# A float32 encoder layer on one core: the second chunk's global attention heads in query blocks of 512 instead of 256

## The chip, the core and the metric

One core of a Trainium2 chip runs the whole program. The metric is the device time of one execution in microseconds (us). The engines are PE (matmuls; PEld is its weight load), DVE (elementwise work on 128 partitions), ACT (activations and copies), POOL (here the reductions over partitions) and SP (issues the DMAs). Each engine goes through its own list of instructions in the order that the build has fixed; semaphores tie the lists together.

## What is computed

Two sequences, 1024 and 256 tokens with 16 meta tokens put before each, go through one layer of width 2048. A norm and one projection give q, k, v and a gate z for 8 global heads (a: 2 shared k and v, with rotary embedding) and 8 local heads (b: a window of 8 x 16 keys with a bias). Then one output projection and the residual. Cut to the part that the change touches, the global attention:

```python
qg = qb.reshape(B, L, N_KV_A, G, HEAD_DIM)
s = jnp.einsum('blkgd,bskd->bkgls', qg, k).astype(jnp.float32) * scale
p = jax.nn.softmax(s, axis=-1).astype(v.dtype)
o = jnp.einsum('bkgls,bskd->blkgd', p, v)
...
ya = global_gqa(qa, ka, va) * jax.nn.silu(za)
```

## The kernel before, in words

Float32 products are made of three: each operand is split into a high part that PE takes as it is and a low remainder, and high x high, high x low and low x high are summed in PSUM. `split` (L64) does this with an ACT copy (`hi`, L66) and a DVE subtraction (`lo`, L67).

The tokens are worked in two chunks: chunk one holds the short sequence, the first 240 tokens of the long one and the meta tokens; chunk two the other 784 tokens. The projection goes by strips of 128 output columns (`strips`, L192): for each of 16 tiles of the model width and each of two token blocks (512 and 272 in chunk two) three matmuls (L227 to L229) add to a PSUM tile `pp`, of which there are 4, so two strips of chunk two fit. A strip is then evacuated: `qk_evac` (L257) for q and k, with up to six tiles of the pool `ev` for each block (8 tiles in all), `z_evac` (L299) for the gate, `v_rows` and `rows_out` (L287, L530) for v.

Chunk two's global heads are the loop in `chunk2` (L941 to L953): for each of the 8 heads a strip for z, one for q, then `run` (L879), which attends, then `fill`, which puts one strip of the local heads behind as filling. There is one tile each for k, v, q and z (one buffer), so the next head's q can be written only when this head's last score matmul has read it. `run` calls `attend` (L366) for four blocks of 256 queries. A block has 8 key tiles of 128; two of them share one PSUM bank (`sp`, 2 banks) and one score buffer (`S`, pool `s`, 5 buffers of 128 x 512):

- scores: three matmuls for each key tile (L377 to L379), an ACT copy to `S` (L381), a running maximum on DVE from the second pair on (L385, L387); then two matmuls for the meta keys (`meta_scores`, L312; Sl on ACT at L319, Sm on DVE at L320);
- maximum over the two halves (L392) and with the meta scores (L326), then over the partitions on POOL (L328);
- probabilities: subtraction on DVE (L397), exponential on ACT (L398), sum on DVE (L401, L403, L407, L343) and over the partitions on POOL (L346);
- values: each pair's probabilities are split into `ph` and `pl` (2 buffers each, pool `ph`), and three matmuls for each key tile (L418 to L420) and one for the meta values (L421) add to `po`; `put_y` (L349) divides by the sum, multiplies by the gate and stores.

Behind the global heads come the local heads (`attend_strip`, L463), tied to fixed places in the remaining strips, and then the output projection (L1068 to L1070).

The order on each engine is not written out by hand: the build simulates the engines with its own costs and lists each engine's instructions as they come free there, by the order of the code, with buffers and banks limiting what may run ahead. So changed tiles and buffers move instructions on every engine. The pools are opened in `build` (L1187): `work` (L1225) lists those that both kinds of attention share, L1236 opens them for the whole of chunk two.

## Time and profile before

| | |
|---|---|
| median of 3 runs | 2160.92 us (2160.66 to 2160.97) |
| profiled execution: its time | 2159.27 us |
| profiled execution: span | 2157.5 us |
| matmuls on PE | 11745 |
| first and last score matmul of the wide stage (L377) start at | 686.8 us and 1313.9 us |
| DVE busy in 760 to 840, 840 to 920, 920 to 1000 us | 75.03, 74.62, 73.24 of 80 us |
| ACT busy in the same | 60.19, 60.69, 58.92 of 80 us |
| clock granted to PE, mean | 1.00 |

How to read the views: busy time counts an instruction from its start to its end, and neighbours on one engine can overlap; PE's ends are modelled, so the distance from one matmul's start to the next says more than its duration. A row of groups gives line, engine, operation, the tiles written and read, shapes and count, then busy us and mean ns, then the engine's idle time ahead of them and what ended it. In the timeline a row is start, length, engine, line, operation; x4 means four such instructions in a row, taken together. The stage of the change runs from 686 to 1316 us.

### The profile page before, as it was taken

The page shows a single profiled execution, that of the slowest core. Times are in us where ns is not written, and L with a number is a line of the kernel's source. Part 1 is how long each engine was busy: PE and PEld are TensorE (multiplying, and loading weights), DVE is VectorE, ACT ScalarE, POOL GpSimd, SP SyncE. Part 2 cuts the span into 40 slices and gives each one's busy share as a digit, 9 for nine tenths or more (in the row PEclk, how much of TensorE's full clock was granted, in tenths as well). Part 3 has the DMA queues.
Part 4 walks back from the last instruction along what each step waited for, and adds up shares of the span by engine and source line. Part 5 has one row for each costly group of instructions (what it writes and reads, how often), then busy time and mean ns, then how long its engine had stood idle before and what let it go on. Part 6 is the DMA issues. An engine that isn't in the chain of part 4 may idle for free.

```text
span 2157.5 us, 33972 instructions
## 1 busy us (share of the span) xinstructions
PE 2151.3 (100%) x11745; PEld 1877.5 (87%) x11745; DVE 1658.5 (77%) x2989; ACT 1189.0 (55%) x2411; POOL 522.3 (24%) x250
## 2 busy tenths in 40 slices
PE   9999999999999999999999999999999999999999
PEld 7888888888888999999999999998989988888887
DVE  7698976788874899997799998677787886545763
ACT  7677644454565777776677775444443464232230
POOL 1142422222221223231143224324333311000000
PEclk9999999999999999999999999999999999999999
DMA  8666789988664333334332344654443364662663
GB/s 294 216 192 221 241 297 313 331 288 265 214 193 137 94 105 104 106 105 135 98 107 93 104 127 146 188 158 136 130 132 123 115 212 142 239 235 92 234 224 108
DMA packets 257420, 377.24 MB, mean 175 GB/s; under 512 B 43072, under 2 KB 108768, under 8 KB 257248
## 3 DMA queue, kind: packets, MB, share of 16 engines
q1 hardware_dynamic: 257248, 375.07, 53.6%
q8 instruction: 92, 1.51, 0.3%
q14 instruction: 80, 0.66, 0.1%
HBM read 281.01 MB, written 100.38 MB: 177 GB/s over the span
## 4 chain that ended last, share of the span: by engine, by line
PE 99%; DMA 0%; DVE 0%; SPq 0%; issue 0%; ACT 0%
PE pp L227 22%; PE pp L229 22%; PE pp L228 22%; PE pq L1069 6%; PE pq L1068 6%; PE pq L1070 6%; PE po L519 2%; PE sp L485 2%; PE sp L378 1%; PE sp L379 1%; PE sp L377 1%; PE po L420 1%; PE po L419 1%; PE po L418 1%; PE tp L540 0%; PE sp L430 0%
## 5 line engine op out<-in xcount | busy, mean ns | idle before, releaser
L227 PE MATMUL pp<-x,wh 128*128 128x512 f32 (+1 forms) x1664 | 655.0, 395 | 0.9 <-ACT wh L66 0.9
L229 PE MATMUL pp<-x,wl 128*128 128x512 f32 (+1 forms) x1664 | 647.6, 390 | 0.0
L228 PE MATMUL pp<-x,wh 128*128 128x512 f32 (+1 forms) x1664 | 647.1, 389 | 0.0
L229 PEld LDWEIGHTS pp<-x,wl 128*128 128x128 f32 x1664 | 312.4, 188 | 60.9 <-DVE wl L67 0.2
L227 PEld LDWEIGHTS pp<-x,wh 128*128 128x128 f32 x1664 | 312.3, 188 | 59.0 <-ACT wh L66 3.1
L228 PEld LDWEIGHTS pp<-x,wh 128*128 128x128 f32 x1664 | 312.8, 188 | 52.1
L67 DVE TENSOR_TENSOR wl<-wr,wh 128x512 fp32r<-128x512 f32 (+2 forms) x287 | 215.5, 753 | 122.2 <-ACT wh L66 91.3
L262 POOL PARTITION_ALL_REDUCE m<-ms x78 | 222.4, 2852 | 354.3 <-ACT ms L260 293.1
L346 POOL PARTITION_ALL_REDUCE tot<-a x80 | 179.2, 2240 | 435.4 <-DVE a L343 417.1
L66 ACT CAST wh<-wr 128x512 fp32r<-128x512 f32 (+2 forms) x287 | 173.7, 610 | 184.2 <-PE pp L228 170.4
L228 PE MATMUL pp<-xb,wh 128*128 128x272 f32 x832 | 240.7, 289 | 0.0
L227 PE MATMUL pp<-xb,wh 128*128 128x272 f32 x832 | 239.8, 288 | 0.0
L229 PE MATMUL pp<-xb,wl 128*128 128x272 f32 x832 | 239.1, 287 | 0.0
L328 POOL PARTITION_ALL_REDUCE ma<-m x80 | 114.4, 1429 | 448.4 <-DVE m L326 439.7
L1068 PE MATMUL pq<-wm,yh 128*128 128x512 f32 x560 | 218.3, 390 | 0.0
L1070 PE MATMUL pq<-wm,yl 128*128 128x512 f32 x560 | 218.2, 390 | 0.0
L1069 PE MATMUL pq<-wm,yh 128*128 128x512 f32 x560 | 218.0, 389 | 0.0
L227 PEld LDWEIGHTS pp<-xb,wh 128*128 128x128 f32 x832 | 156.5, 188 | 7.5
L228 PEld LDWEIGHTS pp<-xb,wh 128*128 128x128 f32 x832 | 156.5, 188 | 7.5
L229 PEld LDWEIGHTS pp<-xb,wl 128*128 128x128 f32 x832 | 157.4, 189 | 0.3
L1068 PEld LDWEIGHTS pq<-wm,yh 128*128 128x128 f32 x560 | 105.1, 188 | 21.8
L1070 PEld LDWEIGHTS pq<-wm,yl 128*128 128x128 f32 x560 | 105.1, 188 | 21.8
(214 smaller groups left out, 3932.1 us busy)
## 6 DMA issues: line engine op xcount, KB each, us to landing
wr<-in_w_in SPq DMA_DIRECT2D x413, 256.0 KB, 3.4
wld<-wl SPq DMA_DIRECT2D x132, 256.0 KB, 4.2
wl<-wld SPq DMA_DIRECT2D x132, 256.0 KB, 3.1
yr<-yd SPq DMA_DIRECT2D x35, 512.0 KB, 5.1
wq<-in_w_out SPq DMA_DIRECT2D x64, 256.0 KB, 5.0
td<-wq SPq DMA_DIRECT2D x64, 256.0 KB, 4.4
ww<-td SPq DMA_DIRECT2D x64, 256.0 KB, 5.2
ww<-in_w_out SPq DMA_DIRECT2D x48, 256.0 KB, 5.4
```

The source lines that it names most:

```text
L66: self.hi = nc.scalar.copy(hi, full).ins
L67: return nc.vector.tensor_tensor(out=lo, in0=full, in1=hi.bitcast(F32), op=ALU.subtract).ins
L227: nc.tensor.matmul(p[:, :n], wh[:, k, :], xh[:, :n], start=first, stop=False)
L228: nc.tensor.matmul(p[:, :n], wh[:, k, :], xl[:, :n], start=False, stop=False)
L229: self.lastmm = nc.tensor.matmul(p[:, :n], wl[:, k, :], xh[:, :n], start=False, stop=last).ins
L262: nc.gpsimd.partition_all_reduce(m2[:], ms[:], P, RED.add)
L328: nc.gpsimd.partition_all_reduce(ma[:], m1[:], P, RED.max)
L346: nc.gpsimd.partition_all_reduce(tot[:], a1[:], P, RED.add)
L485: nc.tensor.matmul(dst, k[:, o:o + P], qfv[:, a:e, :], start=True, stop=True)
L1068: nc.tensor.matmul(ps, yh, wh, start=k == 0, stop=False)
L1069: nc.tensor.matmul(ps, yh, wl, start=False, stop=False)
L1070: self.lastmm = nc.tensor.matmul(ps, yl, wh, start=False, stop=k == 7).ins
```

## The change

`run` calls a new function, `attend_wide`, for two blocks of 512 queries (`WB`) instead of `attend` for four of 256. Each key tile has a PSUM bank and a score buffer of its own, so that every matmul of these heads has 512 columns, and there is no halving step at the end of maximum and sum. The low parts `pl` are taken from the score buffers (`s`, now 9 buffers of the same size), the high parts `ph` keep two buffers. `y` is written over the sum's tile. The low meta probabilities have one tile of 512 columns (`Pw`) instead of two of 256. The wide heads' pools are closed before the local heads begin, and the local heads open theirs on the same memory. `po` has 512 columns everywhere, of which the others use 256. The diff, cut to its core:

```diff
@@ meta_scores
+        n = pm.shape[1]
+        sm = self.sm.tile([M3, n], F32, tag="Sm", name="Sm")
+        if n > QB:
+            sl = self.ph.tile([P, n], F32R, tag="ph", name="Sl", align_bytes=ALIGN)[:M3].bitcast(F32)
+        else:
+            sl = self.t.tile([P, n], F32, tag="t", name="Sl")[:M3]
...
@@ meta_probs
-        pm3 = self.pms[self.npm % 2]
+        pm3 = self.pms[self.npm % len(self.pms)]
...
@@ put_y
-        y = self.y.tile([P, QB], F32, tag="y", name="y")
+        y = tot if n > QB else self.y.tile([P, n], F32, tag="y", name="y")
...
+    def attend_wide(self, q, zs, keys, meta, vals, vmeta, ydst):
+
+        nc = self.nc
+        qh, ql = q[:, 0, :], q[:, 1, :]
+        S, mx = [], None
+
+        def bank(name):
+            return self.sp.tile([P, 2, QB], F32, tag="sp", name=name)[:].rearrange("p a b -> p (a b)")
+
+        for j, (kh, kl) in enumerate(keys):
+            ps = bank("sp")
+            nc.tensor.matmul(ps, kh, qh, start=True, stop=False)
+            nc.tensor.matmul(ps, kh, ql, start=False, stop=False)
+            nc.tensor.matmul(ps, kl, qh, start=False, stop=True)
+            s = self.s.tile([P, WB], F32, tag="S", name="S", align_bytes=ALIGN)
+            nc.scalar.copy(s[:], ps)
+            S.append(s)
+            if j == 1:
+                mx = self.mx.tile([P, WB], F32, tag="mx", name="mx")
+            if j:
+                nc.vector.tensor_tensor(out=mx[:], in0=(S[0] if j == 1 else mx)[:], in1=ps, op=ALU.max)
+        sm = self.meta_scores(bank("sm_ps"), meta, qh, ql, 1.0)
+        ma = self.all_max(mx, sm)
+        for j, s in enumerate(S):
+            nc.vector.tensor_tensor(out=s[:], in0=s[:], in1=ma[:], op=ALU.subtract)
+            nc.scalar.activation(s[:], s[:], AF.Exp, scale=SCALE)
+            if j == 1:
+                acc = self.mx.tile([P, WB], F32, tag="mx", name="acc")
+            if j:
+                nc.vector.tensor_tensor(out=acc[:], in0=(S[0] if j == 1 else acc)[:], in1=s[:], op=ALU.add)
+        pm3 = self.meta_probs(sm, ma, SCALE)
+        tot = self.all_sum(acc, sm)
+        po = self.op.tile([P, WB], F32, tag="po", name="po")[:]
+        for j, (s, (vh, vl)) in enumerate(zip(S, vals)):
+            ph = self.ph.tile([P, WB], F32R, tag="ph", name="ph", align_bytes=ALIGN)
+            pl = self.s.tile([P, WB], F32R, tag="S", name="pl", align_bytes=ALIGN)[:]
+            self.split(ph[:], pl, s[:])
+            nc.tensor.matmul(po, vh, ph[:], start=j == 0, stop=False)
+            nc.tensor.matmul(po, vl, ph[:], start=False, stop=False)
+            nc.tensor.matmul(po, vh, pl, start=False, stop=False)
+        nc.tensor.matmul(po, vmeta, pm3[:], start=False, stop=True)
+        self.put_y(po, tot, zs, ydst)
...
@@ chunk2, run
-            for b in range(4):
-                c = slice(QB * b, QB * b + QB)
+            for b in range(2):
+                c = slice(WB * b, WB * b + WB)
                 keys = [(k[:, 0, o:o + P], k[:, 1, o:o + P]) for o in range(0, NP, P)]
-                for _ in self.attend(q[:, :, c], z[:, c], keys, km, v, vm[:], self.yd[0][:, 2 * b:2 * b + 2, h, :]):
-                    pass
+                self.attend_wide(q[:, :, c], z[:, c], keys, km, v, vm[:], self.yd[0][:, 4 * b:4 * b + 4, h, :])
...
+        self.open_local()
         for f in (load_kq, load_v, load_z):
...
@@ build
-                for name, bufs in (("k", 1), ("v", 1), ("tab", 1), ("q", 1), ("z", 1), *work, ("y", 2), ("qf", 1)):
-                    pool(es_attn, name, bufs, **kw)
+                first = (("k", 1), ("v", 1), ("tab", 1), ("q", 1), ("z", 1))
+                es_wide = ExitStack()
+                for name, bufs in (*first, ("s", 9), ("mx", 2), ("t", 3), ("ph", 2), ("sm", 1), ("pw", 1)):
+                    pool(es_wide, name, bufs, **kw)
...
```

The order of instructions changes with it. PE at the end of global head 4 (counted from 0), from the meta scores (`sm_ps`) of its last block on; before (`pp` is a strip's PSUM, `x` and `xb` its tokens, `wh` and `wl` its weights):

```order
L315 MATMUL sm_ps_12031<-q_11445,km_10978 112x256
L316 MATMUL sm_ps_12031<-q_11445,km_10978 112x256
L227 MATMUL pp_13071<-x_6705,wh_13075 128x512
L228 MATMUL pp_13071<-x_6705,wh_13075 128x512
L229 MATMUL pp_13071<-x_6705,wl_13076 128x512
L227 MATMUL pp_13072<-xb_6682,wh_13075 128x272
L228 MATMUL pp_13072<-xb_6682,wh_13075 128x272
L229 MATMUL pp_13072<-xb_6682,wl_13076 128x272
L227 MATMUL pp_13072<-xb_6690,wh_13075 128x272
L228 MATMUL pp_13072<-xb_6690,wh_13075 128x272
L229 MATMUL pp_13072<-xb_6690,wl_13076 128x272
L227 MATMUL pp_13072<-xb_6698,wh_13075 128x272
```

and now, where `sp` is already the next head's scores (`q_11550`), `po` the sum of the values, and `ph` and `pl` the split probabilities:

```order
L316 MATMUL sm_ps_11157<-q_10764,km_10297 112x512
L317 MATMUL sm_ps_11157<-q_10764,km_10297 112x512
L441 MATMUL sp_11724<-q_11550,kf_10294 128x512
L441 MATMUL sp_11730<-q_11550,kf_10294 128x512
L442 MATMUL sp_11724<-q_11550,kf_10294 128x512
L443 MATMUL sp_11724<-q_11550,kf_10294 128x512
L442 MATMUL sp_11730<-q_11550,kf_10294 128x512
L443 MATMUL sp_11730<-q_11550,kf_10294 128x512
L467 MATMUL po_11198<-ph_11199,va_10616 128x512
L468 MATMUL po_11198<-ph_11199,va_10617 128x512
L469 MATMUL po_11198<-pl_11200,va_10616 128x512
```

Before, a strip's matmuls stand behind the meta scores, and the block's own first value matmul comes 82 rows behind the first of them; now it stands directly behind the next head's first six score matmuls, and the next strip's matmuls come behind the values.

DVE at the same place, the last rows up to the block's last low part; before (`acc` is the running sum, `Pm` the low meta probabilities, `a1` the sum of the halves, `mx` the next block's maximum; `t`, `rs_l` and `rs_r0` belong to the evacuation of a strip):

```order
L67 TENSOR_TENSOR pl_12076<-S_12007,ph_12075 128x512
L274 TENSOR_TENSOR t_12555<-t_12555,ts_12557 128x272
L403 TENSOR_TENSOR acc_12047<-acc_12047,S_12028 128x512
L338 TENSOR_TENSOR Pm_270<-Sm_12034,Pm_270 16x256
L407 TENSOR_TENSOR a1_12059<-acc_12047 128x256
L385 TENSOR_TENSOR mx_12593<-S_12582,sp_12584 128x512
L343 TENSOR_TENSOR a1_12059<-a1_12059,Sm_12034 16x256
L81 TENSOR_TENSOR rs_l_12565<-m2_12552,rs_l_12565 128x272
L67 TENSOR_TENSOR pl_12086<-S_12018,ph_12085 128x512
L82 SCALAR_TENSOR_TENSOR rs_r0_12567<-rs_l_12565,rs_r0_12567 128x272
L277 TENSOR_TENSOR rs_r0_12567<-t_12555,rs_r0_12567 128x272
L67 TENSOR_TENSOR pl_12096<-S_12028,ph_12095 128x512
```

and now:

```order
L68 TENSOR_TENSOR pl_11221<-S_11126,ph_11220 128x512
L459 TENSOR_TENSOR acc_11171<-acc_11171,S_11133 128x512
L82 TENSOR_TENSOR rs_l_12177<-m2_12174,rs_l_12177 128x512
L68 TENSOR_TENSOR pl_11228<-S_11133,ph_11227 128x512
L459 TENSOR_TENSOR acc_11171<-acc_11171,S_11140 128x512
L68 TENSOR_TENSOR pl_11235<-S_11140,ph_11234 128x512
L83 SCALAR_TENSOR_TENSOR rs_r0_12179<-rs_l_12177,rs_r0_12179 128x512
L459 TENSOR_TENSOR acc_11171<-acc_11171,S_11147 128x512
L68 TENSOR_TENSOR pl_11242<-S_11147,ph_11241 128x512
L264 TENSOR_TENSOR m2_12188<-m2_12188,eb2_321 128x272
L281 SCALAR_TENSOR_TENSOR rs_r0_12179<-pp_12050,nqkw_245,rs_r0_12179 128x512
L68 TENSOR_TENSOR pl_11249<-S_11154,ph_11248 128x512
```

The four low parts of a block have become eight, and the evacuation of the waiting strip (`pp_12050`) stands between them.

More of the change, by code (lines that the diff above doesn't have):

```diff
@@ L351, in put_y @@
         nc = self.nc
[L352 removed]
+        n = tot.shape[1]
+        r = self.t.tile([P, n], F32, tag="t", name="r")
         nc.scalar.activation(r[:], tot[:], AF.Ln)
@@ new lines, in attend @@
+        nc.tensor.matmul(po, vmeta, pm3[:], start=False, stop=True)
[37 more added lines that the diff above has]
+            nc.tensor.matmul(po, vh, pl, start=False, stop=False)
+        nc.tensor.matmul(po, vmeta, pm3[:], start=False, stop=True)
@@ L456, in attend_sample @@
         yield
-        po = self.op.tile([P, QB], F32, tag="po", name="po")
-        nc.tensor.matmul(po[:], vmeta, pm3[:], start=True, stop=False)
+        po = self.op.tile([P, WB], F32, tag="po", name="po")[:, :QB]
+        nc.tensor.matmul(po, vmeta, pm3[:], start=True, stop=False)
         for i in range(2):
@@ L514, in attend_strip @@
         yield
-        po = self.op.tile([P, QB], F32, tag="po", name="po")
-        nc.tensor.matmul(po[:], vmeta, pm3[:], start=True, stop=False)
+        po = self.op.tile([P, WB], F32, tag="po", name="po")[:, :QB]
+        nc.tensor.matmul(po, vmeta, pm3[:], start=True, stop=False)
         for t in (0, 3, 1, 2):
@@ L565, in meta_tiles @@
         self.npm = 0
-        self.pms = [self.mt.tile([P, QB], F32R, tag=f"Pm{i}", name="Pm") for i in range(2)]
+        self.pms = self.pms_narrow = [self.mt.tile([P, QB], F32R, tag=f"Pm{i}", name="Pm") for i in range(2)]
         self.vm3s = [self.mt.tile([P, P], F32R, tag="vm", name="vm3")]
@@ L1235, in build, with open_local @@
                 pool(es_proj, "ev", 8, side="right", **kw)
-                for name, bufs in (("k", 1), ("v", 1), ("tab", 1), ("q", 1), ("z", 1), *work, ("y", 2), ("qf", 1)):
-                    pool(es_attn, name, bufs, **kw)
+                first = (("k", 1), ("v", 1), ("tab", 1), ("q", 1), ("z", 1))
+                es_wide = ExitStack()
+                for name, bufs in (*first, ("s", 9), ("mx", 2), ("t", 3), ("ph", 2), ("sm", 1), ("pw", 1)):
+                    pool(es_wide, name, bufs, **kw)
+                self.pms = [self.pw.tile([P, WB], F32R, tag="Pw", name="Pm")]
+                nc.gpsimd.memset(self.pms[0][:].bitcast(F32), 0.0)
+                def open_local():
+                    es_wide.close()
+                    self.pms = self.pms_narrow
+                    for name, bufs in (*first, *(x for x in work if x[0] != "ph"), ("y", 2), ("qf", 1)):
+                        pool(es_attn, name, bufs, **kw)
+                self.open_local = open_local
                 self.chunk2()
```

25 lines of the change are left out of this document (11 added, 14 removed).

## The prediction

> **What bounds the kernel now.** I read the page first, then the list of waits, then the stage of the change in the table of stretches, then single instructions in the timeline. The profiled execution took 2159.27 us, 1.77 more than its span of 2157.5. First line of the page, and the chain that ended last by engine:
>
> ```profile
> PE 2151.3 (100%) x11745; PEld 1877.5 (87%) x11745; DVE 1658.5 (77%) x2989; ACT 1189.0 (55%) x2411; POOL 522.3 (24%) x250
> PE 99%; DMA 0%; DVE 0%; SPq 0%; issue 0%; ACT 0%
> ```
>
> All that PE ever waited for, of the whole run, in the view of the waits (total, times, longest):
>
> ```profile
> PE warm L633 <- DVE wz L630: 1.2, 1, 1.2
> PE pp L227 <- ACT wh L66: 0.9, 2, 0.6
> PE tp L296 <- DVE vt L289: 0.3, 1, 0.3
> ```
>
> PE bounds every stage; nothing else ever holds it up. So the change can gain only by shortening PE's own work, and loses each microsecond by which PE now waits. Chunk two's global heads, then its local heads, in the table of stretches (length; busy time and count of PE, PEld, DVE, ACT, POOL):
>
> ```profile
> 686.00:1316.00 630.00, 630.00 (x4089) 577.39 (x4088) 551.75 (x1002) 453.00 (x917) 175.43 (x88) 1.00 0.35 106
> 1320.00:1800.00 480.00, 480.00 (x2840) 431.70 (x2839) 373.51 (x793) 226.94 (x506) 163.31 (x87) 1.00 0.48 153
> ```
>
> DVE is busy 551.75 of 630 us (88%): it keeps up, with little to spare. What matters is how much other work PE has in its queue while an attention block passes through DVE.
>
> **Part by part. The wider matmuls.** Counts by form, before (the first and the last of six like rows, L418 to L420 and L377 to L379):
>
> ```profile
> L420 PE MATMUL po<-pl,va 128*128 128x256 f32 x256 | 71.9, 281 | 0.0
> ...
> L377 PE MATMUL sp<-q,kf 128*128 128x256 f32 x256 | 70.8, 282 | 0.0
> ```
>
> With the three meta matmuls of each of the 32 blocks (L315, L316, L421) that is 6 x 256 + 96 = 1632 matmuls of 256 columns; they become 816 of 512. Durations overlap, so the price is the distance of starts, in the timeline:
>
> ```profile
> 1171.80 0.40 PE L228 MATMUL pp<-x,wh 128*128 128x512 f32 x1
> ...
> 1173.88 0.39 PE L228 MATMUL pp<-x,wh 128*128 128x512 f32 x1
> ...
> 1175.34 0.28 PE L378 MATMUL sp<-q,kf 128*128 128x256 f32 x1
> ...
> 1175.94 0.28 PE L378 MATMUL sp<-q,kf 128*128 128x256 f32 x1
> ```
>
> Nine steps of 512 columns in 2.08 us are 0.231 each; five of 256 in 0.60 are 0.120. A pair saves 0.009 us, 816 pairs 7 us (5 to 9, as starts are given to 0.01 us). The Trainium skill, TensorE: Matmul & The Clock Gate, section Back-to-back issue gap, gives N / 2.4 + 2.5 ns, by which a pair would save 2.5 ns and all pairs 2 us; the distances above show more, and the measurement decides.
>
> **The waits that come in.** A block now holds eight score buffers through subtraction, exponential and split; nine exist, and each low part takes one. The next block's first scores need the buffer of this block's eighth tile, so blocks follow one another instead of overlapping. The last score copies of the next head stand behind the last split, and that head's q, of which there is one tile, is written only when this head's last scores are done. A strip's results then queue for the eight ev tiles behind q's, its PSUM banks stay taken, and PE has no projection to run. The order of instructions shows the outcome. Behind the last score matmul of the second block of heads 1, 4 and 5 (counted from 0) PE has only the next head's first six score matmuls and then the value matmuls, each waiting for DVE; the first projection is the 33rd instruction. Before, projections stood there.
>
> How long until DVE releases it? From the meta scores to the seventh low part stand Sl on ACT and 33 DVE instructions: 29 of 512 elements, 4 of 272, the same in the three places. Durations, by form in the stretch of these heads:
>
> ```profile
> L67 DVE TENSOR_TENSOR pl<-S,ph 128x512 fp32r<-128x512 f32 x124 | 91.6, 750 | 7.0 <-ACT ph L66 4.3 <-PE po L420 2.5
> L397 DVE TENSOR_TENSOR S<-S,ma 128x512 f32<-128x512 f32 x124 | 78.6, 696 | 6.2 <-POOL ma L328 6.0
> L403 DVE TENSOR_TENSOR acc<-acc,S 128x512 f32<-128x512 f32 x62 | 45.6, 735 | 1.2 <-ACT S L398 0.8
> L387 DVE TENSOR_TENSOR mx<-mx,sp 128x512 f32<-128x512 f32 x64 | 43.7, 682 | 18.2 <-ACT S L381 17.3
> L82 DVE SCALAR_TENSOR_TENSOR rs_r<-rs_l,rs_r 128x512 f32<-128x512 f32 x13 | 11.8, 911 | 0.3
> L263 DVE TENSOR_TENSOR m<-m,eb 128x512 f32<-128x512 f32 x13 | 9.7, 750 | 0.0
> L81 DVE TENSOR_TENSOR rs_l<-m,rs_l 128x512 f32<-128x512 f32 x13 | 9.5, 727 | 3.3 <-ACT rs_l L80 3.3
> L277 DVE TENSOR_TENSOR rs_r<-t,rs_r 128x272 f32<-128x272 f32 x8 | 7.1, 885 | 0.1
> L81 DVE TENSOR_TENSOR rs_l<-m,rs_l 128x272 f32<-128x272 f32 x13 | 6.5, 499 | 2.0 <-ACT rs_l L80 2.0
> L67 DVE TENSOR_TENSOR q<-rs_r,q 128x272 fp32r<-128x272 f32 x7 | 5.9, 847 | 0.7 <-ACT q L66 0.7
> L82 DVE SCALAR_TENSOR_TENSOR rs_r<-rs_l,rs_r 128x272 f32<-128x272 f32 x12 | 5.1, 427 | 0.0
> ```
>
> By these means: 8 subtractions 5.6, 7 low parts 5.3, 6 sums 4.4, 5 small ones of 512 columns (taken as L387) 3.4, L263, L81 and L82 2.4, the four of 272 columns 2.7, together 23.8 us; Sl adds 0.58 (the copy of 128x512 below), 24.3 in all. The four of 272 cover the all-reduce of the maximum, estimated at twice the 1.37 us of 256 columns at most:
>
> ```profile
> L381 ACT COPY S<-sp 128x512 f32<-128x512 f32 x126 | 72.8, 581 | 47.8 <-PE sp L379 43.3 <-DVE pl L67 3.2
> L328 POOL PARTITION_ALL_REDUCE ma<-m x31 | 42.5, 1372 | 131.0 <-DVE m L326 122.3 <-ACT wh L211 5.2 <-DMA wl<-wld 3.5
> ```
>
> Means hold overlap: DVE starts come closer. One block of before in the timeline, from its meta scores to its last low part:
>
> ```profile
> 1143.79 0.28 PE L316 MATMUL sm_ps<-q,km 128*112 128x256 f32 x1
> ...
> 1144.96 0.41 DVE L320 SCALAR_TENSOR_TENSOR Sm<-sm_ps,Sl 48x256 f32<-48x256 f32 x1
> 1145.29 0.41 DVE L392 TENSOR_TENSOR m<-mx 128x256 f32<-128x256 f32 x1
> ...
> 1147.55 2.50 DVE L397 TENSOR_TENSOR S<-S,ma 128x512 f32<-128x512 f32 x4
> 1149.97 0.41 DVE L333 TENSOR_TENSOR Sm<-Sm,ma 48x256 f32<-48x256 f32 x1
> ...
> 1161.91 0.68 DVE L67 TENSOR_TENSOR pl<-S,ph 128x512 fp32r<-128x512 f32 x1
> ```
>
> Four subtractions in 2.42 us are 0.605 each, 256 columns 0.33. At that pace the 33 take 29 x 0.605 + 4 x 0.35 = 18.9 us, with Sl and some 0.6 of the all-reduce left open 20.1. The block shown decides which is nearer: from L320 on it has 17 instructions of 512 columns and 10 of 256, 13.6 us by starts, 16.4 by means; it took 17.6. So I take the means. PE's work up to there is 29 matmuls at 0.231, 6.7 us. PE stands 24.3 - 6.7 = 17.6 us, at least 20.1 - 6.7 = 13.4. I take 17, three times: 51 us (40 to 54).
>
> The same count for the other 13 blocks: PE's queue is short by 4.6, 3.6, 4.6 and 2.0 us in the second blocks of heads 0, 2, 3 and 6 by means, by 0.6, 0, 1.5 and 0 by starts: 2 to 15 us, and I take 8, the middle, since waits in so short a gap may also fall elsewhere. In the other nine blocks PE has 3.6 to 5.7 us to spare by means, so they cost nothing while that cover holds. Counted so, every block of before has 1.6 us or more to spare, which fits its empty list of waits.
>
> After a stop PE may start slowly. At the kernel's start nine matmuls of 512 columns show it:
>
> ```profile
> 1.17 4.02 PE L633 MATMUL warm<-wz 128*128 128x512 bf16 x9 [1.17 <-DVE wz L630]
> ```
>
> That is 0.447 each instead of 0.231, 1.9 us lost on nine. I put 2 us on each of the three long stops, 6 us (0 to 9: during a stop a value matmul runs now and then). The Trainium skill, TensorE: Matmul & The Clock Gate, section Why this matters for your kernels, says that a gap of some 3 us between bursts puts PE back to half its clock; the nine matmuls agree with a half clock at the start, and no run here shows it after a gap yet.
>
> **Edits put at nothing.** DVE's sums and maxima go from 2 x 3 to 7 instructions, but the halves' L392 and L407 go away and the instructions on few partitions halve in number; all is off PE's chain except where counted. One Pm tile instead of two: its next writer comes a block later, some 40 us. The local heads' own pools wait for the wide ones; their first scores stand 46 us of PE work behind the last wide scores. Local heads now start later and share less time: DVE is 78% busy there (373.51 of 480), and in the order their scores still lead their values by 15 us of PE work or more, but for the last head, whose order stays as it was. If that cover failed I would add 10 us.
>
> **Sum.** 2159.3 - 7 + 51 + 8 + 6 = 2217.3 for the profiled execution; the median of the runs lies 1.65 us above it (2160.92), so 2219.
>
> **Rivals.** First, the waits are covered and only the matmuls count: 2160.9 - 7 = 2154, faster. Before's rows speak for it (PE never waited, though DVE was as busy), the order speaks against it: PE and DVE each go through their queue in order, so 6.7 us of PE work can hide at most as much of DVE's. It decides from the point where DVE gets to the seventh low part within 6.7 us. Chance 0.04; another 0.02 for gain and waits that cancel within 0.2%.
>
> Second, DVE goes at its pace of starts and the short gaps close by themselves: - 9 + 40 with no slow start, 2160.9 + 31 = 2192 and up to 2203. For it: DVE has no one to wait for in the three places. Against: the block shown took 17.6. Chance 0.22.
>
> Third, the ring of nine buffers makes first blocks wait as well. They have 3.6 to 5.7 us to spare by means; if DVE's own waits, which made the block shown 1.2 us longer than its means, grow with twice the tiles and more to 7 us, eight blocks lose some 2 to 3 each, 20 us: 2239 and above. Chance 0.14.
>
> My forecast, 2204 to 2238, has 0.58.
>
> **How the numbers follow.** A measurement of this kernel tells a difference from none at about 0.2%, 4.3 us. The range takes in the second rival and the lower part of the third: 2190 to 2249, where 2249 is the forecast with 20 us of the third rival and 10 for a lost cover in the local heads. Slower holds 0.94, same 0.02, faster 0.04.
>
> **What would show it.** Right: PE waits for DVE's pl and ACT's ph in three groups of stops, some 17 us in each, at heads 1, 4 and 5; starts of 512-column attention matmuls 0.23 apart; the stage 686 to 1316 longer by 40 us or more for the same work; PE's busy share below 100% there. Wrong: an empty list of waits of PE; stops at every block; or stops in the local heads.

## The result, and the profile after

Before 2160.84 us (median; 2159.80 to 2162.29), after 2252.33 us (2249.91 to 2255.86): the ratio is 1.0425, with an interval of 1.0411 to 1.0438. The change makes the kernel 91.5 us slower; the forecast was 58 us slower, and the time lies 3 us outside its range. The profiled execution took 2255.86 us, its span is 2254.0; it is the slowest of the six and lies 96.6 us above the profiled execution before.

First line of the page after, and the chain that ended last by engine:

```profile
PE 2185.6 (97%) x10929; PEld 1849.7 (82%) x10929; DVE 1659.5 (74%) x2813; ACT 1181.7 (52%) x2331; POOL 520.2 (23%) x219
...
PE 87%; DVE 6%; ACT 2%; issue 2%; DMA 2%; POOL 1%; SPq 0%; DVEq 0%; POOLq 0%; ACTq 0%
```

DVE's busy time is what it was (1658.5 before): nothing was added to its work, and yet it now has 6% of the chain. What PE waited for, in the view of the waits after (total, times, longest):

```profile
PE po L469 <- DVE pl L68: 17.0, 15, 3.0
PE sp L441 <- DMA q<-qd: 12.7, 4, 3.3
PE po L467 <- ACT ph L67: 12.1, 3, 4.4
PE pp L228 <- ACT ts L271: 6.7, 2, 5.8
PE sp L441 <- ACT rs_l L81: 3.0, 1, 3.0
PE sm_ps L316 <- DVE mx L450: 2.8, 6, 0.6
```

Where before had a list of three waits of 1.2 us at most, there are waits for low and high parts (the forecast stops), and others that the forecast did not have: the first score of a head waits for the DMA of its q, and a strip waits for its PSUM bank (`ts` is the evacuation). The table of stretches after, in 40 us (length; busy time and count of PE, PEld, DVE, ACT, POOL; PE's granted clock; the DMA share; GB/s):

```profile
840.00:880.00 40.00, 29.09 (x119) 21.36 (x117) 28.48 (x42) 22.13 (x41) 7.05 (x3) 0.80 0.22 62
...
1160.00:1200.00 40.00, 26.84 (x109) 19.17 (x109) 36.20 (x57) 25.10 (x49) 10.53 (x4) 0.83 0.11 35
...
1240.00:1280.00 40.00, 27.46 (x98) 19.12 (x97) 30.14 (x45) 21.04 (x41) 7.29 (x3) 0.75 0.16 47
```

In the slices of the three long stops PE is busy for 27 to 29 of 40 us, at a mean clock of 0.75 to 0.83; and DVE, for which it waits, has only 28 to 36 of 40. Closer stretches at head 1, the 20 us ahead of the last meta score and the stop itself, show how that goes together:

```profile
840.00:860.00 20.00, 19.36 (x99) 15.82 (x97) 9.93 (x14) 8.46 (x15) 2.02 (x1) 1.00 0.37 105
860.33:883.61 23.28, 12.56 (x28) 7.10 (x29) 21.82 (x34) 15.89 (x30) 8.56 (x3) 0.63 0.05 12
```

Ahead of the stop PE is busy and DVE stands half of the time (9.93 of 20 us); in the stop DVE is nearly full (21.82 of 23.28) and PE stands. The two take turns.

How a long stop runs is seen at the end of head 1 (from 0), in the timeline after, from the last meta score to the seventh low part:

```profile
859.93 0.40 PE L317 MATMUL sm_ps<-q,km 128*112 128x512 f32 x1
860.99 0.68 DVE L325 SCALAR_TENSOR_TENSOR Sm<-sm_ps,Sl 48x512 f32<-48x512 f32 x1 [0.48 <-ACT Sl L324]
...
863.04 1.78 POOL L333 PARTITION_ALL_REDUCE ma<-mx  x1 [21.02 <-DVE mx L331]
863.23 1.15 DVE L82 TENSOR_TENSOR rs_l<-m,rs_l 128x272 f32<-128x272 f32 x1 [0.36 <-ACT rs_l L81]
...
864.88 0.44 DVE L278 TENSOR_TENSOR rs_r<-t,rs_r 128x272 f32<-128x272 f32 x1
...
865.16 3.26 POOL L263 PARTITION_ALL_REDUCE m<-ms  x1 [0.34 <-ACT ms L261]
...
865.81 1.91 DVE L68 TENSOR_TENSOR q<-rs_r,q 128x272 fp32r<-128x272 f32 x1 [0.48 <-ACT q L67]
867.65 4.89 DVE L454 TENSOR_TENSOR S<-S,ma 128x512 f32<-128x512 f32 x8
...
873.67 0.67 DVE L68 TENSOR_TENSOR pl<-S,ph 128x512 fp32r<-128x512 f32 x1
...
882.92 0.69 DVE L68 TENSOR_TENSOR pl<-S,ph 128x512 fp32r<-128x512 f32 x1
```

From the end of the meta scores (860.33) to the end of the seventh low part (883.61) pass 23.3 us; the forecast had counted 24.3. PE's work in it is the 6.7 us of the forecast, so the core of the stop is 16.6 us.

A short gap is at the end of head 2, again in the timeline after:

```profile
956.73 0.40 PE L317 MATMUL sm_ps<-q,km 128*112 128x512 f32 x1
957.15 0.53 SPq L867 DMA_DIRECT2D q<-qd  x1
...
960.22 1.19 PE L441 MATMUL sp<-q,kf 128*128 128x512 f32 x2 [3.10 <-DMA q<-qd]
...
961.21 0.63 PE L442 MATMUL sp<-q,kf 128*128 128x512 f32 x1
...
961.64 0.63 PE L443 MATMUL sp<-q,kf 128*128 128x512 f32 x1
...
965.91 0.55 PE L229 MATMUL pp<-x,wh 128*128 128x512 f32 x1
...
966.30 0.40 PE L230 MATMUL pp<-x,wl 128*128 128x512 f32 x1
966.53 0.39 PE L228 MATMUL pp<-x,wh 128*128 128x512 f32 x1
```

Directly behind the meta scores PE comes to the next head's first score. Its q can only be fetched when the single q tile is free (957.15), so PE stands for 3.1 us. After that its starts are 0.43 apart instead of 0.23 until 965.91, 5.7 us long; the granted clock was 0.50 there (row in the last section). The forecast put nothing on such a gap behind a wait of 3 us.

For the balance I add up, over all of PE's starts, by how much the distance to the next start exceeds the usual one (0.227 us for 512 columns, 0.125 for 272, 0.119 for 256, 0.163 for 192, 0.112 for 128), where it does so by more than 0.05 us, waits and slow starts together, and call it lost PE time. From 640 to 1400 us it is 3.3 us before and 96.6 after: 22.2, 19.7 and 20.5 in the long stops at heads 1, 4 and 5, and 6.9, 8.8, 9.6 and 7.7 in the short gaps at the ends of heads 0, 2, 3 and 6; 16.5 of it all is slow starts. Behind 1400 us, in the local heads, it is 8.6 before and 17.6 after. That is 102.3 us more; the spans differ by 96.5, so by this balance the wider matmuls gave back 5.8.

### The profile page after: what moved, and what is told of

Read it like the earlier page. It is cut to its first block, busy times and chain, and to the rows that moved or that the text cites. A ratio compares the mean times of both kernels' runs of the same rounds, so it can differ in the third digit from the quotient of the medians.

```text
span 2254.0 us, 31981 instructions
## 1 busy us (share of the span) xinstructions
PE 2185.6 (97%) x10929; PEld 1849.7 (82%) x10929; DVE 1659.5 (74%) x2813; ACT 1181.7 (52%) x2331; POOL 520.2 (23%) x219
## 4 chain that ended last, share of the span: by engine, by line
PE 87%; DVE 6%; ACT 2%; issue 2%; DMA 2%; POOL 1%; SPq 0%; DVEq 0%; POOLq 0%; ACTq 0%
PE pp L228 20%; PE pp L229 19%; PE pp L230 19%; PE pq L1119 6%; PE pq L1117 6%; PE pq L1118 6%; PE sp L441 1%; PE sp L443 1%; PE sp L442 1%; PE sp L534 1%; PE po L469 1%; PE po L568 1%; PE po L468 1%; PE po L467 1%; POOL m L263 1%
## 5 line engine op out<-in xcount | busy, mean ns | idle before, releaser
L263 POOL PARTITION_ALL_REDUCE m<-ms x78 | 233.9, 2999 | 458.9 <-ACT ms L261 353.1
L68 DVE TENSOR_TENSOR wl<-wr,wh 128x512 fp32r<-128x512 f32 (+2 forms) x287 | 209.7, 732 | 95.5 <-ACT wh L67 71.8
L67 ACT CAST wh<-wr 128x512 fp32r<-128x512 f32 (+2 forms) x287 | 173.9, 611 | 173.8 <-PE pp L229 148.9
L351 POOL PARTITION_ALL_REDUCE tot<-a x48 | 117.8, 2454 | 200.1 <-DVE a L348 187.6
L333 POOL PARTITION_ALL_REDUCE ma<-m x48 | 75.5, 1572 | 251.4 <-DVE m L331 251.4
L450 DVE TENSOR_TENSOR mx<-mx,sp 128x512 f32<-128x512 f32 x96 | 65.8, 685 | 88.4 <-ACT S L445 86.7
L445 ACT COPY S<-sp 128x512 f32<-128x512 f32 x128 | 73.2, 585 | 106.5 <-PE sp L443 106.0
```

Of the source, the lines that this page charges most:

```text
L67: self.hi = nc.scalar.copy(hi, full).ins
L68: return nc.vector.tensor_tensor(out=lo, in0=full, in1=hi.bitcast(F32), op=ALU.subtract).ins
L263: nc.gpsimd.partition_all_reduce(m2[:], ms[:], P, RED.add)
L333: nc.gpsimd.partition_all_reduce(ma[:], m1[:], P, RED.max)
L351: nc.gpsimd.partition_all_reduce(tot[:], a1[:], P, RED.add)
L445: nc.scalar.copy(s[:], ps)
```

## The experiments

Theory A, at the start: PE has no projection to run at a head's end, because two strips stand in all four PSUM banks until q, z and the ev tiles come free. Rivals: the DMA of q, the ring of nine score buffers (R), a DVE chain that is too long for any order (C), POOL's reductions (P), the closing of the pools (K); L and O came up on the way. Where an expectation counts how far "PE's queue is short", it counts as the prediction did, with mean durations, in that kernel's own order.

| | | median us | ratio to before, interval |
|---|---|---|---|
| 1 | q in half tiles | 2250.22 | 1.0417 (1.0401 to 1.0432) |
| 2 | own low parts, one mx buffer | 2226.41 | 1.0305 (1.0290 to 1.0320) |
| 3 | nine ev tiles, one mx buffer | 2244.42 | 1.0387 (1.0371 to 1.0402) |
| 4 | q and z halves, blocks cut at 272, own low parts, one mx buffer | 2210.73 | 1.0230 (1.0212 to 1.0247) |
| 5 | narrow blocks, buffers of before, pools closed | 2162.27 | 1.0010 (1.0001 to 1.0019) |
| 6 | narrow blocks in the change's pools | 2236.25 | 1.0353 (1.0337 to 1.0368) |
| 7 | q and z halves, blocks cut at 272 | 2226.75 | 1.0311 (1.0294 to 1.0328) |
| 8 | reductions left out | 2241.76 | 1.0380 (1.0364 to 1.0395) |
| 9 | own low parts, two mx buffers | 2160.76 | 1.0002 (0.9993 to 1.0011) |
| 10 | 9 with q and z halves, cut at 272 | 2166.31 | 1.0027 (1.0017 to 1.0037) |
| 11 | 6 with own low parts | 2166.41 | 1.0028 (1.0016 to 1.0040) |
| 12 | one mx buffer | 2253.52 | 1.0431 (1.0416 to 1.0445) |
| 13 | 9 with the low parts in the ring, ten buffers | 2248.53 | 1.0411 (1.0395 to 1.0427) |
| 14 | 9 with shared pools kept open | 2160.64 | 1.0003 (0.9994 to 1.0012) |

**1. The DMA of q.**

```diff
-            q = self.q.tile([P, 2, NP], F32R, tag="q", name="q", align_bytes=ALIGN)
-            nc.sync.dma_start(q[:, :, :C1P].bitcast(F32), self.qd[h][:])
+            q = [self.q.tile([P, 2, WB], F32R, tag="q", name="q", align_bytes=ALIGN) for _ in range(2)]
+            nc.sync.dma_start(q[0][:, :, :C1P].bitcast(F32), self.qd[h][:])
...
```

> The next head's q goes into two half tiles, so its first half can be written when this head's first block has been scored; buffers, banks and memory are the same otherwise. Theory A (PE runs out of projections at a head's end, because two strips stand in all four PSUM banks until q, z and the ev tiles come free; and in the short gaps it waits for the DMA of q on top of that): the 12.7 us that PE waited for q's DMA leave the list of waits, with some 8 us of slow starts behind them; the three long stops stay, since counted in the order PE's queue is still 17 us short at heads 1, 4 and 5; part of the short gaps stays as waits for DVE's pl (4.4, 3.5, 4.6 and 3.4 us by mean durations). 2240, from 2232 to 2248. Rival D (the DMA of q is a bystander, PE would have waited for DVE's chain as long): 2249 to 2255. Rival Q (the one q tile alone makes all the stops): 2190 or less.

Measured 2250.22. The first waits of PE in this kernel:

```profile
PE po L467 <- ACT ph L67: 21.5, 3, 7.2
PE po L469 <- DVE pl L68: 18.2, 16, 3.0
PE pp L228 <- ACT ts L271: 5.9, 1, 5.9
PE pp L228 <- DVE z L303: 5.1, 2, 2.5
```

The DMA has gone from the list, and its 12.7 us have gone to the block's own parts and to the strips' banks; the four short gaps still lose 5.9, 7.0, 8.7 and 7.0 us. Rival D holds: the DMA was the wait that happened to end last.

**2, 3 and 4. Low parts, ev tiles, all together.** Experiment 2 gives the low parts a pool of their own, 3 adds an ev tile; both pay with a buffer of `mx`, which holds the running maximum and the running sum. Experiment 4 adds the half tiles of 1, the same for z, and the token blocks (0, 272), (272, 512):

```diff
-            pl = self.s.tile([P, WB], F32R, tag="S", name="pl", align_bytes=ALIGN)[:]
+            pl = self.plo.tile([P, WB], F32R, tag="pl", name="pl", align_bytes=ALIGN)[:]
...
-                for name, bufs in (*first, ("s", 9), ("mx", 2), ("t", 3), ("ph", 2), ("sm", 1), ("pw", 1)):
+                for name, bufs in (*first, ("s", 8), ("mx", 1), ("t", 3), ("ph", 2), ("plo", 2), ("sm", 1), ("pw", 1)):
```

```diff
-                pool(es_proj, "ev", 8, side="right", **kw)
+                pool(es_proj, "ev", 9, side="right", **kw)
...
-                for name, bufs in (*first, ("s", 9), ("mx", 2), ("t", 3), ("ph", 2), ("sm", 1), ("pw", 1)):
+                for name, bufs in (*first, ("s", 9), ("mx", 1), ("t", 3), ("ph", 2), ("sm", 1), ("pw", 1)):
```

> The low parts get two buffers of their own; the score buffers go from nine to eight and one buffer of the running maximum goes, to pay for them. Rival R (low parts in the score buffers tie one block to the next, and that makes the stops): with that tie gone the stops go, 2190 or less. Theory A (the strips that stand in the PSUM banks make the stops): counted in the order PE's queue is still 13.9, 13.6 and 17.1 us short at heads 1, 4 and 5, and 3.7, 0.1 and 2.1 us elsewhere, 50 in all where it was 66: 2236, from 2228 to 2246.

> Nine ev tiles for the evacuation of strips instead of eight, paid for with one buffer of the running maximum; q, z, score buffers and low parts as in the changed kernel. Theory A: a strip gets out of its PSUM banks a little earlier, and the order no longer has a place where the next head's projections all stand behind this head's values: by mean durations PE's queue is short by 1.6 us at head 1, 12.0 at head 2, 8.0 at head 3 and 1.8 at head 5, 23 us where it was 66. 2209, from 2198 to 2225. Rival C (DVE's work in a block is too much for any order: what PE does not lose at one place it loses at the next): 2240 to 2255. Rival R (the tie by the score buffers): 2245 to 2255, since that tie is as it was.

> All together: q and z in two half tiles each, the projection's token blocks of chunk two cut at 272 and 512 instead of 512 and 272 so that each fills one half tile, low parts in two buffers of their own, eight score buffers, one buffer of the running maximum. DVE and ACT do the same work as in the changed kernel. Theory A: a strip's first half leaves its bank when the head's first block is done, so projections stand behind nearly every block's meta scores; by mean durations PE's queue is short at one place only, by 4.8 us, so the wide matmuls' 9 us come through: 2158, from 2150 to 2172. Rival C (DVE's chain of eight tiles is too long for any order): 2220 or more. Rival W (wide matmuls save nothing, starts 0.23 apart are a reading error): 2166 to 2180 with next to no waits.

Measured 2226.41, 2244.42 and 2210.73: theory A misses all three (2236, 2209, 2158), the first by little; rival R misses them too (2190 or less in experiment 2), and experiment 4 lies 9 us below C's 2220. In experiment 3 the long stops are gone as counted, but the loss is not: 64.7 us up to 1400, where the count says 23. In experiment 4, with 5 us in the count, it is 40.5, at other instructions. Behind 1400 us, in the local heads, the two lose another 36.6 and 26.4 us where the changed kernel loses 17.6; what makes this is not shown. PE's first waits in experiment 4:

```profile
PE pp L228 <- ACT ts L271: 11.0, 5, 3.7
PE sp L441 <- DVE mx L450: 5.3, 7, 1.5
PE po L469 <- DVE pl L68: 4.2, 4, 1.8
```

A count of low parts against value matmuls, as in my prediction, sees one of three waits: score banks wait for DVE's maximum and strips' banks for ACT. Theory A fell as a sufficient cause; C looked the nearest.

**5 and 6. Without the width.** Both call blocks of 256. Experiment 5 uses the old function with its buffers, in pools that are closed before the local heads; 6 uses the new pools and the new function, written for any width, with two key tiles to a bank (the first diff is 5's pools, the second 6's blocks):

```diff
...
-                for name, bufs in (*first, ("s", 9), ("mx", 2), ("t", 3), ("ph", 2), ("sm", 1), ("pw", 1)):
+                for name, bufs in (*first, *work, ("y", 2)):
                     pool(es_wide, name, bufs, **kw)
...
```

```diff
+BLOCKS = ((0, 256), (256, 256), (512, 256), (768, 256))
...
-            for b in range(2):
-                c = slice(WB * b, WB * b + WB)
+            for o, n in BLOCKS:
+                c, b = slice(o, o + n), o // P
...
```

> The blocks of 256 queries with all the buffers of the kernel before, but with the change's other edits: the pools of these heads are closed before the local heads and opened again for them, and po has 512 columns. Rival K (closing and opening the pools costs the local heads what they lost in the changed kernel): 8 us more than before, 2169. Theory L (blocks of 512 have twice the chain from scores to values, with buffers for less than one block ahead, and that alone makes every loss): as before, 2161, within 4.

> All of the change but the width: four blocks of 256 queries go through the new function and the new pools (two key tiles to a bank and a score buffer, low parts in the nine score buffers, three buffers for ma, tot and r, one for Sm, one Pm tile, y over tot). Theory L (the width makes the loss): a block holds four of the nine score buffers, 2160 to 2172. Rival R (the shared ring and the fewer small buffers make it): counted in the order by mean durations PE's queue is short by 10.3 us at head 1, 4.0 at head 3, 9.9 and 10.9 at heads 4 and 5 and some 8 in small pieces, 43 us in all: 2204, from 2190 to 2225.

Measured 2162.27 and 2236.25. Closing the pools costs some 2 us (0.2 to 4 by the interval), not 8. And most of the loss (76 of 92 us) comes without any wide block: theory L falls, and with it C in the form that a chain of eight tiles of 512 is to blame. R has the direction, but its 2204 (up to 2225) is 11 us short even at its upper end. The two kernels differ in the buffers and in the function that uses them; experiment 11 tells these apart.

**7 and 8. The other half of experiment 4, and the reductions.** Experiment 7 has only the half tiles and the token blocks. Experiment 8:

```diff
...
+        if m1.shape[1] > QB:
+            nc.scalar.copy(ma[:], m1[:])
+        else:
+            nc.gpsimd.partition_all_reduce(ma[:], m1[:], P, RED.max)
...
+        if a1.shape[1] > QB:
+            nc.scalar.activation(tot[:], a1[:], AF.Copy, bias=1.0)
+        else:
+            nc.gpsimd.partition_all_reduce(tot[:], a1[:], P, RED.add)
```

> Of the fourth experiment only the half tiles of q and z and the token blocks cut at 272; low parts, score buffers and the running maximum's buffers as in the changed kernel. The fourth experiment lay 16 us below the second, which had the low parts' own buffers alone. If the two cures add up: 2252 - 16 = 2236, from 2228 to 2243. If each does the whole and they only share it (theory A by its count, 20 us short in the order where it was 66): 2206 or less. If the half tiles do nothing without the low parts' buffers (rival R): 2247 or more.

> Left out of the computation: the maximum and the sum over the partitions of these heads' blocks; an ACT copy of the same size stands in place of each POOL reduction, so each partition uses its own maximum and sum. Theory P (while POOL reduces, DVE is held: in the trace every DVE instruction of these heads that took over 0.93 us, but the one that splits v, ran beside a reduction; the max takes 1.8 us in the chain besides): in each of the seven places some 4 us go, 2225, from 2212 to 2236. Rival N (DVE's own instructions set the stops, the reductions lie beside them): the order is as short as before (16.3 us at heads 1, 4 and 5, and 2.5, 9.5, 1.9 and 9.7): 2246 to 2262.

Measured 2226.75 and 2241.76. The half tiles lie between cures that add up (2236) and theory A (2206): alone they give 26 us, as the own low parts do alone, and both together 42. They look like two ways round one obstacle, though experiments 2 and 4 had also given up a buffer of `mx` (see 9 to 12). Leaving out the reductions gains 10.6 us, between P (27) and N (none), and 85.3 us of lost PE time stay up to 1400: they make the stops longer and do not make them. The instructions are listed in another order there, so the 10.6 are not the price of the reductions alone.

**9 to 12. Both buffers.** Experiment 2's low parts, but `mx` keeps two buffers; the memory comes from the meta probabilities, whose wide tile is now made of the two narrow ones:

```diff
-        self.pms = self.pms_narrow = [self.mt.tile([P, QB], F32R, tag=f"Pm{i}", name="Pm") for i in range(2)]
+        self.pm_wide = self.mt.tile([P, WB], F32R, tag="Pm", name="Pm")
+        self.pms = self.pms_narrow = [self.pm_wide[:, QB * i:QB * i + QB] for i in range(2)]
...
-                for name, bufs in (*first, ("s", 9), ("mx", 2), ("t", 3), ("ph", 2), ("sm", 1), ("pw", 1)):
+                for name, bufs in (*first, ("s", 8), ("mx", 2), ("t", 3), ("ph", 2), ("plo", 2), ("sm", 1)):
```

Experiment 10 adds experiment 7, 11 gives experiment 6 own low parts (seven score buffers and two), 12 is the changed kernel with `("mx", 1)`.

> The low parts get two buffers of their own and the score buffers go from nine to eight, as in the second experiment, but the running maximum keeps its two buffers; the memory comes from the meta probabilities, whose wide tile now is the two narrow ones side by side. Theory O (what the build lists in what order is set by which buffers are shared: low parts that take score buffers put the next block's score copies behind this block's last split, and one buffer for the maximum and the sum put the next block's maxima behind this block's sum, which spoiled the second, third and fourth experiments): counted in the order by mean durations PE's queue is short nowhere by more than 0.5 us: 2160, from 2153 to 2178. Rival C (a wide block's chain on DVE is too long for any order without two blocks overlapping; the fourth experiment was short by 5 us in the count and lost 50): 2200 to 2225.

> The ninth experiment with q and z in half tiles and the token blocks cut at 272, as in the fourth, which had one buffer for the running maximum where this has two. Theory O: PE has 3 us to spare at every block by mean durations, 2156, from 2151 to 2170. Rival C: 2195 to 2212, since nothing in DVE's work differs from the fourth experiment's.

> The sixth experiment (blocks of 256 in the change's pools) with two buffers of their own for the low parts and seven score buffers instead of nine; three buffers for ma, tot and r, one for Sm, one Pm tile, y over tot stay. Theory O: in the order the next block's meta scores again stand ahead of 13 or 17 of this block's 25 value matmuls, where the sixth experiment had none: 2162, from 2157 to 2170. Rival B (the small buffers tie the blocks): 2225 to 2240, as the sixth experiment.

> The changed kernel with one buffer for the running maximum and the running sum instead of two, nothing else: the control for the second, third and fourth experiments, which all had one. Theory O by the order: the places where PE's queue is short are the same as in the changed kernel (17.1 us three times, 4.6, 3.6, 4.6 and 2.0): 2253, from 2246 to 2262; the buffer matters only once the low parts have their own. If one buffer by itself costs what those three lost beyond the count (16 to 60 us): 2268 or more.

Measured 2160.76, 2166.31, 2166.41 and 2253.52. All four lie in theory O's ranges, and C is out: with eight score buffers, two for the low parts and two for maximum and sum the wide blocks lose nothing. Experiment 10, though, came out 5.6 us slower than 9 where theory O had it 4 faster: 3.7 us more of its PE time are lost ahead of 640 us, where strips wait for `x` with the other cut of the token blocks, and as little as in 9 in the global heads (4.0 and 3.9). The four corners: low parts in the ring, 2252 with two mx buffers and 2254 with one; own low parts, 2161 with two and 2226 with one. The second mx buffer is worth 1 us as long as the low parts share, and 66 when they don't (the shared tile of the meta probabilities, which experiments 2 and 12 lack, does little by itself, as 13 shows below). Page and waits of experiment 9, the first waits of the list:

```profile
PE 2149.5 (100%) x10929; PEld 1837.4 (85%) x10929; DVE 1642.8 (76%) x2813; ACT 1176.0 (54%) x2331; POOL 527.4 (24%) x218
```

```profile
PE warm L683 <- DVE wz L680: 1.2, 1, 1.2
PE sp L534 <- ACT wh L67: 1.2, 1, 1.2
```

What DVE does differently is seen in its timeline in experiment 9, amid a block's low parts:

```profile
1146.39 0.68 DVE L450 TENSOR_TENSOR mx<-S,sp 128x512 f32<-128x512 f32 x1
1146.99 0.69 DVE L68 TENSOR_TENSOR pl<-S,ph 128x512 fp32r<-128x512 f32 x1
...
1151.81 0.68 DVE L450 TENSOR_TENSOR mx<-mx,sp 128x512 f32<-128x512 f32 x1
...
1158.31 0.69 DVE L450 TENSOR_TENSOR mx<-mx,sp 128x512 f32<-128x512 f32 x1
1158.92 0.92 DVE L68 TENSOR_TENSOR pl<-S,ph 128x512 fp32r<-128x512 f32 x1
```

The next block's maxima (L450) run between this block's low parts (L68). In the changed kernel the rows from 873.67 to 882.92 are low parts, sums, one step of the meta probabilities and three of a strip's evacuation, and no maximum is among them.

**13 and 14. Ring or shared tile, and the missing gain.** Experiment 13 is 9 with `pl` from pool `s` again and `("s", 10)` for `("s", 8)` and `("plo", 2)`: the same memory. Experiment 14 opens k, v, tab, q, z and mx in the stack that the local heads use, and `qf` first.

> The ninth experiment at the same memory, but the low parts take score buffers again: ten in one ring, where it had eight for the scores and two for the low parts. The meta probabilities' shared tile and both buffers of the maximum are as there. Theory O (that low parts and scores are handed out of one ring, in the order of the code, makes the whole loss): in the order PE's queue is short as in the changed kernel (17.1 us three times, 4.7, 3.7, 5.1 and 2.0): 2251, from 2243 to 2260. If the count of buffers or the shared tile of the meta probabilities had made the difference: 2175 or less.

> The ninth experiment with the pools of k, v, the tables, q, z and the maximum left open for the local heads, and qf opened first, so that the local heads' first scores stand 14 rows behind the last values of the global heads instead of 85. In the ninth experiment PE lost 8 us in small waits and slow starts from 1380 us on, and the pools' closing alone cost 2 us with narrow blocks. Theory (the closing takes back what the wide matmuls save, 816 x 0.007 = 6 us): 2157, from 2154 to 2160. Rival (the local heads are squeezed because the global heads end later, whenever the pools are closed): 2160 to 2163.

Measured 2248.53 and 2160.64. Experiment 13 settles the cause: same memory, same shared tile, ten buffers in one ring instead of eight and two, and the loss is back. Its waits:

```profile
PE sp L441 <- DMA q<-qd: 17.1, 5, 3.9
PE po L469 <- DVE pl L68: 16.9, 16, 3.0
PE po L467 <- ACT ph L67: 10.6, 3, 4.7
```

ACT's rows at the end of head 4 show what the ring does. In experiment 13, the last two high parts of the block (L67) and then the copies of the next head's first scores (L445):

```profile
1174.50 0.62 ACT L67 CAST ph<-S 128x512 fp32r<-128x512 f32 x1 [0.74 <-DVE pl L68]
1176.68 0.62 ACT L67 CAST ph<-S 128x512 fp32r<-128x512 f32 x1 [1.55 <-DVE pl L68]
1177.20 1.07 ACT L445 COPY S<-sp 128x512 f32<-128x512 f32 x2
```

In experiment 9, from the block's third high part to its fourth:

```profile
1103.47 0.62 ACT L67 CAST ph<-S 128x512 fp32r<-128x512 f32 x1 [0.65 <-DVE pl L68]
1104.00 0.58 ACT L445 COPY S<-sp 128x512 f32<-128x512 f32 x1
...
1104.99 0.59 ACT L445 COPY S<-sp 128x512 f32<-128x512 f32 x1
...
1107.47 0.61 ACT L67 CAST ph<-S 128x512 fp32r<-128x512 f32 x1
```

In one ring the next head's score copies come behind this block's last split; with low parts apart they come between the splits. That a ring hands its buffers out in the order of the code, and a low part stands ahead of the next block's scores in the code, would explain it; this step is argued from the order of these rows and not tested by itself.

Experiment 14 hits its rival: the local heads' first score starts at 1369.2 instead of 1381.7 us, and nothing is won. The gain of the wide matmuls in experiment 9 goes like this: lost PE time is 3.9 us up to 1400 (before 3.3) and 14.1 behind it (before 8.6), 6 us more, against 5.8 that the matmuls save. The last value matmul of the global heads comes at 1367.2 us, 30 later than before (1337.2), because more projections (2744 strip matmuls instead of 2548) are used up beside the global heads; the output projection begins at 1762.8, as before (1762.4). So the local heads do the same work in less room, with fewer projections to hide behind; that this costs the 6 us is argued from these times, and no run tests it by itself. No version beat the kernel before.

## Why the prediction was wrong

**The matmuls.** 7 us forecast, 5.8 by the balance: right.

**The three long stops.** 51 and 6 us of slow starts forecast, 62.4 measured. Places and mechanism were right. That the chain of DVE came so near, 23.3 us for 24.3, is in part luck. Up to the first subtraction (860.33 to 867.65) pass 7.3 us where the means give 5.3, since two steps are held beside POOL and DVE waits for ACT; the 25 instructions behind take 16.0 where the means give 19.0, since they go near their pace of starts (eight subtractions in 4.89). The two errors nearly cancel. Missing was what lies around: before the meta scores PE waits for score banks until DVE has taken the maximum (some 1.5 us at head 1), and behind the values a strip waits for its bank (1.8 there).

**The step that failed** is "the same count for the other 13 blocks": 8 us forecast, 33.0 measured (6.9, 8.8, 9.6 and 7.7 at heads 0, 2, 3 and 6). It was mis-sized in three ways. By the means that priced the long stops it gave 14.8 us, but I took 8, the middle between means and starts. 8.7 us are slow starts, which I had put on the long stops only. And it counted low parts against value matmuls alone: at head 0 PE did stand there (five waits for DVE's pl, 3.6 us), but at heads 2 and 6 it stood at the next head's first score (3.1 each) and at head 3 at a strip's first matmul (5.8), which the count did not look at. The term makes 25 of the 38 us by which the profiled execution (96.6 above before) goes beyond the forecast's 58; the local heads make 9 and the long stops 5. Experiments 3, 4 and 7 show the same count failing in the same way.

**Edits put at nothing.** The local heads' cover failed: 9 us, close to the 10 that I named, which was a guess without a working. The pools' closing alone costs some 2 (experiment 5).

**The cause.** "Nine buffers exist, and each low part takes one" named the right edit, but, as experiment 13 shows, for the wrong reason: what counts is the one ring and not the number of buffers. And I took the serial order for a consequence of wide blocks; experiments 6, 9 and 11 show that narrow blocks lose in that ring too (76 us, and 6 outside it) and wide ones lose nothing outside it.

**Rivals.** First blocks never stop (against the third rival); DVE's wide steps did go near the pace of starts, as the second had it, but the chain came out near the means by the held steps, and the short gaps did not close (against the second). The first rival's case, covered waits and 2154, is experiment 9 but for the 6 us that the local heads lose there.

## What to carry to other kernels

When tiles of two steps of a pipeline take their buffers from one pool, ask which step of the next round then stands behind which of this one; at the same memory, a pool for each was worth 88 us here. A queue that is found short at one instruction is short for all that stand behind it: count every wait on that stretch (score banks, strips' banks, DMAs), and a slow start behind each (1.6 to 2.6 us at the four short gaps). And an experiment that pays for one buffer with another can hide its own result: 26 us with the maximum's second buffer given away, 92 with it kept.

## What the runs showed of the hardware

After a gap of 3.1 us at head 2 PE's starts were 0.43 us apart for 5.7 us (960.22 to 965.91). The granted clock (third number from the end) was 0.50 from 959.41 to 966.24, and also from 788.74 to 792.15 at head 0, where PE's longest wait was 1.8 us:

```profile
959.41:966.24 6.83, 6.02 (x14) 4.79 (x15) 5.78 (x11) 4.48 (x10) 1.78 (x1) 0.50 0.02 7
788.74:792.15 3.41, 3.41 (x10) 2.66 (x9) 3.41 (x7) 1.11 (x3) 0.39 (x1) 0.50 0.20 77
```

The Trainium skill, TensorE: Matmul & The Clock Gate, section Why this matters for your kernels, says that idle gaps of more than some 3 us bring the half clock back; the prediction had this open, and the trace agrees for the gap at head 2. At head 0 the half clock came behind five waits of 3.6 us in all, with matmuls between them, so one unbroken gap of 3 us is not the only thing that brings it here; what the condition is, no run shows.

DVE is held beside POOL. In the long stop above a step of 272 columns takes 1.15 us at 863.23 and one takes 1.91 at 865.81, beside reductions of 1.78 and 3.26 us; the step at 864.88, nearly clear of both, takes 0.44. Groups of the stage after show whom it hits (mean ns behind the busy time):

```profile
L68 DVE TENSOR_TENSOR pl<-S,ph 128x512 fp32r<-128x512 f32 x128 | 104.7, 819 | 25.0 <-ACT ph L67 24.5
...
L450 DVE TENSOR_TENSOR mx<-mx,sp 128x512 f32<-128x512 f32 x96 | 65.8, 685 | 88.4 <-ACT S L445 86.7
```

The maximum, which reads one input from PSUM, stays at 685 ns; of the 16 instructions with a PSUM input that ran beside a reduction for over 0.3 us (640 to 1400 us) none took over 0.93 us, of the 94 with both inputs in SBUF 45 did. That is the division of the Trainium skill, SBUF — State Buffer, section Who interferes with whom (a DVE instruction with two SBUF inputs contends with GpSimd's reads). The Trainium skill, SBUF — State Buffer, section SBUF: two separate sides, adds that the one that starts second is blocked for the whole of the first instruction. Here the two held steps ended 0.44 and 0.70 us ahead of the recorded ends of the reductions, so the hold is seen, but not to the very end; spans on POOL are rough.

The maximum over 512 columns took 1.8 us, less than twice the 1.37 of 256, by which I had bounded it; but of the four small steps that were to cover it one was held by it (863.23), and another by the reduction of a strip (865.81).
